# Expert stage of a fused two-block kernel: products split two blocks ahead, one-hots queued behind the products, and a longer pause in the top-k

## The chip, the core and the metric

The kernel runs on one core of a Trainium2 chip. The metric is device time in microseconds (us) of one launch, lower is better; three runs and one profiled execution of the kernel before are given. TensorE is called PE, VectorE DVE, ScalarE ACT, GpSimd POOL.

## The reference, cut to what matters

The program is one transformer block with three mixers and an expert stage, and then two blocks of another kind with four mixers and a feed-forward each. All of it is f32, for 256 tokens of width 1024. The change touches the expert stage alone:

```python
q = (h @ w_q).reshape(b, s, 8, 2, 128)
sc = einsum('bshpc,hpkc->bshpk', q, sub_keys)        # 8 heads x 2 halves x 128 keys
top_v, top_i = top_k(sc, 16)
cand_v = top_v[..., 0, :, None] + top_v[..., 1, None, :]   # 16 x 16 pairs of a head
best_v, best_pos = top_k(cand_v, 16)                 # 16 of 128*128 experts, for each head
gate = softmax(best_v)
act = gelu(einsum('chkd,cd->chk', u_tab[idx], h))
out = einsum('chk,chkd->cd', gate * act, v_tab[idx])
```

## The kernel before, in words

**Everything dense.** Nothing is gathered. The kernel computes act = gelu(U h) for all 16384 experts, as 128 blocks of 128 experts by 256 tokens, a matrix G of gates for all of them (zero for experts that were not picked), and then the sum over blocks of V^T (G * act). The first index of an expert is its block, 0 to 127, the second its row in the block. An f32 product is made of three matmuls on split operands (`mm3`, lines 178 to 180): high part times high part, high times low, low times high. A split is an ACT copy into a rounded type (the high part, line 191) and a DVE subtraction (the low part, line 192).

**Weights.** `Stream` loads weights by DMA on SP and hands them out in slots of eight 128 x 128 blocks. `_slot` splits a slot: `whi` on ACT (line 93), `wlo` on DVE or, where `pool_share` says so, on POOL (line 96). These have high priority, and there are three slots of each. One slot feeds 24 matmuls of 256 columns: one block of U (`u_block`, which ends in a gelu on ACT, line 773), or one block of V (`v_cols` for eight output columns).

**Order.** The scheduler orders each engine's queue at compile time, by priority (order in the program, weights earlier) among the instructions whose inputs it takes to be ready. Each engine runs its queue in order. `issue_after(x)` puts what a block traces on x's engine behind x in that queue; it is an order of issue and no wait. Background work is a generator (`add`). `blks` ticks once for every two weight blocks, so four times a slot; `yield n` asks for the next step after n ticks, rounded up, and `_step` puts the step's PE work behind the last matmul so far. `finish` runs all remaining steps of a task at once.

**Stages of `peer`.** (1) `topk`: eight units (four head pairs by two token halves) are searched on DVE, one per `TK_PACE` = 22 ticks, while PE runs blocks of U (`u_while`) and POOL makes `wlo`. After the last unit it pauses `TK_LAST` ticks. Then `gates` (a DVE subtraction, line 1013; an exp on ACT, line 1015, with a table load; sums and `slg` on DVE, line 1018), 6 ticks, `turn` (PE transposes `ptk`, line 248), 4 ticks. The number of U blocks done by the end is `early`. (2) `build(0, early)`: gates of blocks 0 to 63, in 32 steps of eight tokens. A step makes one-hots on DVE (`e2` line 805, `e1` line 807, `m` = e1 times the gates line 810), multiplies them on PE (`pgb`, line 818, eight matmuls), copies one half on ACT (line 822), adds the other on DVE (line 825) and multiplies it into the acts already there (line 831), or stores it where the act comes later (line 835). `e2`, `e1` and `m` have two buffers each. Meanwhile PE runs 64 blocks of U. (3) `collapse` multiplies gates by late acts, four blocks at a time (line 862), beside `FILL` = 3 blocks of U; blocks done are then `done`. (4) The V loop over blocks b: `weighted(b)` splits G * act into `ga`, of which there are two, and `v_cols` multiplies. After each odd b one block of U runs while any is left. `build(HALF, done)` makes the gates of blocks 64 to 127 beside it, a step per 10 ticks; `weighted(64)` calls `finish` on it, since it needs all tokens.

Of the kernel before, what the change touches and what calls it, by code (L numbers as in the profile page):

```python
# [8 lines left out]
F32R = mybir.dt.float32r  # L9
# [4 lines left out]
ALU = mybir.AluOpType  # L14
# [5 lines left out]
P = 128  # L20
S = 256
# [7 lines left out]
N_HA = 96  # L29
HALF = 64  # L30
TK_PACE = 22
TK_LAST = 48
FILL = 3
T_OH = 8
PACE = {0: 7.5, HALF: 10}
# [2 lines left out]
NBLK = 128  # L38
LAST = 3
# [93 lines left out]
class Core:  # L133
# [614 lines left out]
    def peer(self):  # L748
# [4 lines left out]
        tc, nc, a, ws = self.tc, self.nc, self.a, self.ws  # L753
        with ExitStack() as st:
            p = st.enter_context(tc.tile_pool(name="pe", bufs=1))
            hh, hl = self.hh, self.hl
            i1 = p.tile([P, S], F16, tag="i1", name="i1")
            i2 = p.tile([P, S], F16, tag="i2", name="i2")
            gt = p.tile([P, 2, S], F16, tag="gt", name="gt")
            iot = p.tile([P, P, 2], F16, tag="iot", name="iot")  # L760
            ga = [p.tile([P, 2, S], F32R, tag=f"ga{i}", name="ga") for i in range(2)]
# [22 lines left out]
                u_while(self.topk(tp, i1, i2, gt, iot), HALF, HALF)  # L784
            with tc.tile_pool(name="peg", bufs=1) as gp:
                hb = gp.tile([P, NBLK - N_HA, S], F32, tag="hb", name="hb")
                ws.pool_share = (0, 1)
                n2, n1 = T_OH * P, T_OH * HALF
                e = self.tp.tile([P, 2, n2 + n1], F16, tag="ld", name="e", bufs=1)
                e2s = [e[:, i, 0:n2].rearrange("p (q c r) -> p q c r", c=P, r=2) for i in range(2)]  # L790
                e1s = [e[:, i, n2:n2 + n1].rearrange("p (q c r) -> p q c r", c=HALF, r=2) for i in range(2)]

                def build(c0, done):


                    nq = T_OH // 2

                    def onehots(i):
                        ts = slice(i * T_OH, i * T_OH + T_OH)

                        def bc(x, n):
                            return x[:, ts].rearrange("p (q r) -> p q r", r=2)[:, :, None, :].to_broadcast([P, nq, n, 2])
                        e2, e1 = e2s[i % 2], e1s[i % 2]
                        m = gp.tile([P, nq, 2, HALF, 2], F16, tag="e1g", name="e1g", bufs=2)
                        nc.vector.tensor_tensor(out=e2, in0=iot[:, None].to_broadcast([P, nq, P, 2]), in1=bc(i2, P),
                                                op=ALU.is_equal)
                        nc.vector.tensor_tensor(out=e1, in0=iot[:, None, c0:c0 + HALF].to_broadcast([P, nq, HALF, 2]),
                                                in1=bc(i1, HALF), op=ALU.is_equal)
                        for j in range(2):
                            nc.vector.tensor_tensor(out=m[:, :, j], in0=e1, in1=bc(gt[:, j, :], HALF), op=ALU.mult)  # L810
                        return e2, m

                    def products(i, e2, m):
                        for o in range(0, T_OH, 4):
                            pg = self.bg.tile([P, 4, 2, HALF], F32, tag="bg", name="pgb")
                            for t in range(4):
                                q, r = (o + t) // 2, t % 2
                                nc.tensor.matmul(pg[:, t], lhsT=e2[:, q, :, r], rhs=m[:, q, :, :, r],
                                                 start=True, stop=True)
                            ts = slice(i * T_OH + o, i * T_OH + o + 4)  # L820
                            tmp = self.scr("gs").rearrange("p (t c) -> p t c", c=HALF)
                            nc.scalar.activation(out=tmp, in_=pg[:, :, 0, :], func=AF.Copy)

                            w = min(done, c0 + HALF) - c0
                            nc.vector.tensor_tensor(out=tmp[:, :, 0:w], in0=tmp[:, :, 0:w], in1=pg[:, :, 1, 0:w],
                                                    op=ALU.add)
                            for b, t, c1, c2 in ((ha, 0, 0, N_HA), (hb, N_HA, N_HA, NBLK)):
                                k0, k1 = max(c1, c0), min(c2, c0 + w)
                                if k0 < k1:
                                    d = b[:, k0 - t:k1 - t, ts]  # L830
                                    nc.vector.tensor_tensor(out=d, in0=d, op=ALU.mult,
                                                            in1=tmp[:, :, k0 - c0:k1 - c0].rearrange("p t c -> p c t"))
                                k0, k1 = max(c1, c0 + w), min(c2, c0 + HALF)
                                if k0 < k1:
                                    nc.vector.tensor_tensor(
                                        out=b[:, k0 - t:k1 - t, ts], op=ALU.add,
                                        in0=tmp[:, :, k0 - c0:k1 - c0].rearrange("p t c -> p c t"),
                                        in1=pg[:, :, 1, k0 - c0:k1 - c0].rearrange("p t c -> p c t"))

                    n = S // T_OH  # L840
                    nxt = onehots(0)
                    yield PACE[c0]
                    for i in range(n):
                        cur = nxt
                        if i + 1 < n:
                            nxt = onehots(i + 1)
                        products(i, *cur)
                        yield PACE[c0]

                early = ahead  # L850
                u_while(self.add(build(0, early), unit=1), HALF + early, early)
                assert ahead >= HALF

                def collapse(b0):

                    cut = NBLK - N_HA
                    b1 = min(b0 + 4, HALF)
                    for b, k0, k1 in ((ha, b0, min(b1, cut)), (hb, max(b0, cut), b1)):
                        if k0 < k1:
                            o = HALF if b is ha else HALF - N_HA  # L860
                            with tc.issue_after(ws.on_vector):
                                nc.vector.tensor_tensor(out=ha[:, k0:k1, :], in0=ha[:, k0:k1, :],
                                                        in1=b[:, k0 + o:k1 + o, :], op=ALU.mult)

                def weighted(b, g):

                    if b == HALF:
                        self.finish(more)
                    src = h(b)
                    if b >= done:  # L870
                        with tc.issue_after(ws.on_vector):
                            nc.vector.tensor_tensor(out=src, in0=src, in1=h(b - done), op=ALU.mult)
                    self.split(g[:, 0, :], g[:, 1, :], src)
                    return g


                done = NBLK
                nxt = weighted(0, ga[0])
                late = list(range(early, HALF, 4))
                for i in range(FILL):  # L880
                    for b in late[i * len(late) // FILL:(i + 1) * len(late) // FILL]:
                        collapse(b)
                    u_block(ahead, h(ahead))
                    ahead += 1
                done = ahead
                more = self.add(build(HALF, done), unit=1)
                acc = [pool.tile([P, 2, S], F32, tag=t, name="acc")
                       for pool, t in ((self.mm, "mm"), (self.bg, "bg")) for _ in range(2)]

                def v_cols(c, b, g, first, last):  # L890

                    wh, wl = ws.blks(("v", 0, 0), b, c)
                    self.mm3(acc[c // 2][:, c % 2, :], wh, wl, g[:, 0, :], g[:, 1, :],
                             first and c % 2 == 0, last and c % 2 == 1)

                for b in range(NBLK - LAST):
                    cur = nxt
                    if b + 1 < NBLK - LAST:
                        nxt = weighted(b + 1, ga[(b + 1) % 2])
                    for c in range(KD):  # L900
                        v_cols(c, b, cur, b == 0, False)
                    if b % 2 and ahead < NBLK:
                        u_block(ahead, h(ahead - done))
                        ahead += 1
                assert ahead == NBLK
                tl = self.tp.tile([P, LAST, 2, S], F32R, tag="ld", name="tail", bufs=1)
                tail = [weighted(NBLK - LAST + i, tl[:, i]) for i in range(LAST)]
            with tc.tile_pool(name="per", bufs=1) as gp:
# [6 lines left out]
                for c in range(KD):  # L915
                    for i, g in enumerate(tail):
                        v_cols(c, NBLK - LAST + i, g, False, i == LAST - 1)
                    if c % 2:
                        for d in (c - 1, c):
                            xc = self.x[:, d, :]  # L920
                            nc.vector.scalar_tensor_tensor(out=xc, in0=acc[d // 2][:, d % 2, :], scalar=1.0 / G_SCALE,
                                                           in1=xc, op0=ALU.mult, op1=ALU.add)
# [720 lines left out]
```

## Time and profile before

| | us |
|---|---|
| median of 3 runs | 2073.24 |
| lowest, highest run | 2063.41, 2077.04 |
| profiled execution, its time | 2076.68 |
| profiled execution, its span | 2074.9 |
| top-k beside U blocks | about 308 to 490 |
| `build(0)` beside U blocks (first to last `pgb`) | 500.05 to 685.84 |
| V loop | 694 to 1125 |
| of it with `build(HALF)` (first to last `pgb`) | 703.93 to 942.94 |

The span is the time from the first to the last instruction of the profile; the profiled execution's time is 1.8 us longer. A row of a timeline is start, duration, engine, line, operation, output<-inputs, shapes, count, and in brackets how long the engine sat idle before it and what it waited for. Ends of matmuls are modelled, so the distance of starts tells more than durations.

### The profile page before, as it was taken

The page shows a single profiled execution, that of the slowest core. Times are in us where ns is not written, and L with a number is a line of the kernel's source. Part 1 is how long each engine was busy: PE and PEld are TensorE (multiplying, and loading weights), DVE is VectorE, ACT ScalarE, POOL GpSimd, SP SyncE. Part 2 cuts the span into 40 slices and gives each one's busy share as a digit, 9 for nine tenths or more (in the row PEclk, how much of TensorE's full clock was granted, in tenths as well). Part 3 has the DMA queues.
Part 4 walks back from the last instruction along what each step waited for, and adds up shares of the span by engine and source line. Part 5 has one row for each costly group of instructions (what it writes and reads, how often), then busy time and mean ns, then how long its engine had stood idle before and what let it go on. Part 6 is the DMA issues. An engine that isn't in the chain of part 4 may idle for free.

```text
span 2074.9 us, 41467 instructions
## 1 busy us (share of the span) xinstructions
PE 2022.9 (97%) x16818; PEld 1966.0 (95%) x16818; DVE 1680.6 (81%) x3290; ACT 1158.1 (56%) x1906; POOL 265.4 (13%) x169
## 2 busy tenths in 40 slices
PE   8999999998999999999999999999999999999999
PEld 7989999998999999889999989999999989999997
DVE  7877779999999999886567999977555999977554
ACT  5688654445555555444556665466545666466543
POOL 2201207881000000000000111200000111200000
PEclk9999999999999999999999999999999999999999
DMA  6444555454544444444554643555555644554554
GB/s 213 143 132 170 199 204 173 173 183 143 183 168 178 167 179 178 148 164 163 202 184 182 221 148 142 199 184 187 199 199 188 226 158 144 197 189 166 202 201 152
DMA packets 57019, 370.01 MB, mean 178 GB/s; under 512 B 6587, under 2 KB 10236, under 8 KB 13564
## 3 DMA queue, kind: packets, MB, share of 16 engines
q1 hardware_dynamic: 50256, 357.06, 47.9%
q10 hardware_dynamic: 6572, 10.31, 1.7%
q8 instruction: 131, 2.15, 0.4%
q14 instruction: 60, 0.49, 0.1%
HBM read 364.73 MB, written 2.62 MB: 177 GB/s over the span
## 4 chain that ended last, share of the span: by engine, by line
PE 69%; DVE 19%; ACT 2%; issue 2%; POOL 0%; ACTq 0%; DVEq 0%; POOLq 0%
PE mm L180 5%; PE mm L178 5%; PE mm L179 5%; PE acc L179 5%; PE acc L180 5%; PE acc L178 5%; PE pu L178 4%; PE pu L179 4%; PE pu L180 3%; PE pg L180 3%; PE pg L178 3%; PE pg L179 3%; DVE wlo L96 3%; PE pp L180 2%; PE pp L179 2%; PE pp L178 2%
## 5 line engine op out<-in xcount | busy, mean ns | idle before, releaser
L93 ACT ACTIVATE whi<-raw 128x1024 fp32r<-128x1024 f32 x677 | 717.1, 1060 | 756.9 <-PE acc L179 174.0
L96 DVE TENSOR_TENSOR wlo<-raw,whi 128x1024 fp32r<-128x1024 f32 x622 | 769.1, 1237 | 299.4 <-ACT whi L93 297.6
L178 PE MATMUL pu<-hh,whi 128*128 128x256 f32 x1024 | 290.6, 284 | 6.7 <-ACT whi L93 6.7
L180 PE MATMUL pu<-hh,wlo 128*128 128x256 f32 x1024 | 286.3, 280 | 1.8 <-POOL wlo L96 1.8
L180 PE MATMUL mm<-hh,wlo 128*128 128x256 f32 x1008 | 281.6, 280 | 6.0 <-DVE wlo L96 6.0
L179 PE MATMUL pu<-hl,whi 128*128 128x256 f32 x1024 | 286.4, 280 | 0.0
L178 PE MATMUL mm<-hh,whi 128*128 128x256 f32 x1008 | 281.7, 280 | 0.0
L179 PE MATMUL mm<-hl,whi 128*128 128x256 f32 x1008 | 281.0, 279 | 0.0
L179 PE MATMUL acc<-ga,whi 128*128 128x256 f32 x1000 | 267.5, 281 | 10.0 <-DVE ga L192 10.0
L180 PE MATMUL acc<-ga,wlo 128*128 128x256 f32 x1000 | 264.6, 279 | 0.0
L178 PE MATMUL acc<-ga,whi 128*128 128x256 f32 x1000 | 233.6, 280 | 3.9 <-ACT ga L191 3.9
L179 PEld LDWEIGHTS acc<-ga,whi 128*128 128x128 f32 x1000 | 188.9, 189 | 13.0 <-DVE ga L192 13.0
L178 PEld LDWEIGHTS pu<-hh,whi 128*128 128x128 f32 x1024 | 194.0, 189 | 7.2 <-ACT whi L93 7.1
L180 PEld LDWEIGHTS mm<-hh,wlo 128*128 128x128 f32 x1008 | 190.9, 190 | 9.1 <-DVE wlo L96 7.8
L178 PE MATMUL pg<-hh,whi 128*128 128x256 f32 x704 | 197.7, 281 | 0.2 <-ACT gth L622 0.2
L180 PE MATMUL pg<-hh,wlo 128*128 128x256 f32 x704 | 197.0, 280 | 0.2 <-DVE wlo L96 0.2
L179 PE MATMUL pg<-hl,whi 128*128 128x256 f32 x704 | 196.8, 280 | 0.0
L180 PEld LDWEIGHTS pu<-hh,wlo 128*128 128x128 f32 x1024 | 194.8, 190 | 2.1 <-POOL wlo L96 2.1
L179 PEld LDWEIGHTS pu<-hl,whi 128*128 128x128 f32 x1024 | 193.7, 189 | 0.0
L178 PEld LDWEIGHTS mm<-hh,whi 128*128 128x128 f32 x1008 | 190.9, 189 | 1.2 <-issue 0.7
L179 PEld LDWEIGHTS mm<-hl,whi 128*128 128x128 f32 x1008 | 190.9, 189 | 1.1 <-issue 0.8
L180 PEld LDWEIGHTS acc<-ga,wlo 128*128 128x128 f32 x1000 | 188.6, 189 | 0.0
(413 smaller groups left out, 4862.8 us busy)
## 6 DMA issues: line engine op xcount, KB each, us to landing
raw<-in_w SPq DMA_DIRECT2D x336, 1024.0 KB
raw<-in_w SPq DMA_DIRECT2D x5, 512.0 KB
bias<-bias_scr ACTq DMA_DIRECT2D x4, 512.0 KB
bias_scr<-sbb ACTq DMA_DIRECT2D x16, 96.0 KB
cl<-in_cstl ACTq DMA_DIRECT2D x2, 576.0 KB
x<-in_xT SPq DMA_DIRECT2D x4, 256.0 KB
memt<-in_memT ACTq DMA_DIRECT2D x1, 1024.0 KB
keys<-in_keysT ACTq DMA_DIRECT2D x1, 1024.0 KB
```

The lines of the kernel that those rows point to most:

```text
L93: self.on_scalar = nc.scalar.activation(out=hi, in_=src, func=AF.Copy).ins
L96: i = eng.tensor_tensor(out=lo, in0=src, in1=hi.bitcast(F32), op=ALU.subtract)
L178: mm(out, lhsT=wh, rhs=xh, start=start, stop=False)
L179: mm(out, lhsT=wh, rhs=xl, start=False, stop=False)
L180: self.on_pe = mm(out, lhsT=wl, rhs=xh, start=False, stop=stop).ins
```

## The change

- `TK_LAST` goes from 48 to 64 ticks.
- A third `ga` buffer. `weighted` is called for block 1 ahead of the V loop and for block b + 2 at the head of iteration b (before: block b + 1).
- In a build step the products of step i come first in the program, then the one-hots of step i + 1 (before: the other way round), and the `e2` comparison of step i + 1 is queued behind the last DVE instruction of the products of step i. `e1` and `m` get no such tie.

```diff
-TK_LAST = 48
+TK_LAST = 64
...
+                ga.append(gp.tile([P, 2, S], F32R, tag="ga2", name="ga"))
...
+                    used = []
...
                         m = gp.tile([P, nq, 2, HALF, 2], F16, tag="e1g", name="e1g", bufs=2)
-                        nc.vector.tensor_tensor(out=e2, in0=iot[:, None].to_broadcast([P, nq, P, 2]), in1=bc(i2, P),
-                                                op=ALU.is_equal)
+                        with ExitStack() as st:
+                            if used:
+                                st.enter_context(tc.issue_after(used[-1]))
+                            nc.vector.tensor_tensor(out=e2, in0=iot[:, None].to_broadcast([P, nq, P, 2]),
+                                                    in1=bc(i2, P), op=ALU.is_equal)
...
-                                    nc.vector.tensor_tensor(out=d, in0=d, op=ALU.mult,
-                                                            in1=tmp[:, :, k0 - c0:k1 - c0].rearrange("p t c -> p c t"))
+                                    used.append(nc.vector.tensor_tensor(
+                                        out=d, in0=d, op=ALU.mult,
+                                        in1=tmp[:, :, k0 - c0:k1 - c0].rearrange("p t c -> p c t")).ins)
...
-                        cur = nxt
+
+                        products(i, *nxt)
                         if i + 1 < n:
                             nxt = onehots(i + 1)
-                        products(i, *cur)
...
-                nxt = weighted(0, ga[0])
+                ready = [weighted(0, ga[0])]
...
+                ready.append(weighted(1, ga[1]))
                 for b in range(NBLK - LAST):
-                    cur = nxt
-                    if b + 1 < NBLK - LAST:
-                        nxt = weighted(b + 1, ga[(b + 1) % 2])
+                    if b + 2 < NBLK - LAST:
+                        ready.append(weighted(b + 2, ga[(b + 2) % 3]))
+                    cur = ready.pop(0)
```

## Rows read from the trace of the kernel before

**Rows 1.** The page, busy time of each engine over the whole span.
```profile
PE 2022.9 (97%) x16818; PEld 1966.0 (95%) x16818; DVE 1680.6 (81%) x3290; ACT 1158.1 (56%) x1906; POOL 265.4 (13%) x169
```

**Rows 2.** Waits of PE, 475 to 1130: total us, times, longest.
```profile
PE acc L179 <- DVE ga L192: 10.0, 15, 1.1
PE pu L178 <- ACT whi L93: 6.7, 2, 6.0
PE acc L178 <- ACT ga L191: 3.9, 1, 3.9
PE pu L180 <- POOL wlo L96: 1.8, 1, 1.8
```

**Rows 3.** Windows: length, busy us (instructions) by engine, granted clock, DMA share, GB/s.
```profile
425.00:450.00 25.00, 25.00 (x214) 25.00 (x213) 24.73 (x65) 11.87 (x18) 20.19 (x10) 1.00 0.47 169
475.00:500.00 25.00, 17.48 (x126) 16.82 (x126) 23.95 (x60) 11.81 (x22) 7.67 (x3) 0.80 0.37 127
525.00:675.00 150.00, 150.00 (x1404) 149.11 (x1403) 142.22 (x301) 80.39 (x152) 0.00 (x0) 1.00 0.49 176
825.00:925.00 100.00, 91.89 (x818) 89.09 (x818) 87.80 (x205) 48.72 (x86) 0.00 (x0) 1.00 0.44 159
```

**Rows 4.** Timeline of ACT at the end of the top-k.
```profile
470.16 1.28 ACT L1015 ACT_TABLE_LOAD   x1
478.92 0.31 ACT L1015 ACTIVATE ge<-ge 128x128 f32<-128x128 f32 x1 [7.47 <-DVE ge L1013]
```

**Rows 5.** Timeline of PE at the end of the top-k.
```profile
480.23 0.58 PE L178 MATMUL pu<-hh,whi 128*128 128x256 f32 x1 [6.02 <-ACT whi L93]
...
489.89 0.33 PE L248 MATMUL ptk<-cst,slg 128*128 128x128 f32 x1 [0.52 <-DVE slg L1018]
```

**Rows 6.** Timeline of DVE, last two units of the top-k.
```profile
455.76 2.31 DVE L978 TENSOR_TENSOR cd<-tv 128x128 f32<-128x128 f32 x1
...
476.11 0.27 DVE L978 TENSOR_TENSOR cd<-tv 128x128 f32<-128x128 f32 x1
...
478.61 0.27 DVE L1013 TENSOR_TENSOR ge<-bv 128x128 f32<-128x128 f32 x1
```

**Rows 7.** Timeline of PE, gate products of both builds.
```profile
679.85 0.63 PE L818 MATMUL pgb<-e1g,e 128*128 128x128 f16 x8
...
685.84 0.63 PE L818 MATMUL pgb<-e1g,e 128*128 128x128 f16 x8
...
703.93 0.64 PE L818 MATMUL pgb<-e1g,e 128*128 128x128 f16 x8
...
825.53 0.64 PE L818 MATMUL pgb<-e1g,e 128*128 128x128 f16 x8
...
933.56 0.63 PE L818 MATMUL pgb<-e1g,e 128*128 128x128 f16 x8
...
939.55 0.63 PE L818 MATMUL pgb<-e1g,e 128*128 128x128 f16 x8
```

**Rows 8.** Timeline of DVE, the last steps of the first build, and collapse.
```profile
680.52 0.69 DVE L805 TENSOR_TENSOR e<-iot,i 128x1024 f16<-128x1024 f16 x1 [0.31 <-PE pgb L818]
681.12 0.75 DVE L810 TENSOR_TENSOR e1g<-e,gt 128x512 f16<-128x512 f16 x2
...
683.82 0.41 DVE L807 TENSOR_TENSOR e<-iot,i 128x512 f16<-128x512 f16 x1
...
684.99 1.22 DVE L96 TENSOR_TENSOR wlo<-raw,whi 128x1024 fp32r<-128x1024 f32 x1
...
690.98 4.95 DVE L862 TENSOR_TENSOR ha<-ha,hb 128x1024 f32<-128x1024 f32 x5
```

**Rows 9.** Timeline of DVE, products of a step at the end of the second build.
```profile
941.87 0.36 DVE L825 TENSOR_TENSOR gs<-gs,pgb 128x200 f32<-128x200 f32 x1
...
943.53 0.27 DVE L831 TENSOR_TENSOR hb<-hb,gs 128x72 f32<-128x72 f32 x1
```

**Rows 10.** Waits of DVE, 475 to 1130: total us, times, longest.
```profile
DVE e L805 <- PE pgb L818: 30.6, 53, 1.7
```

More of the change, by code (lines that the diff above doesn't have):

```diff
@@ L830, in products @@
                                     d = b[:, k0 - t:k1 - t, ts]
-                                    nc.vector.tensor_tensor(out=d, in0=d, op=ALU.mult,
-                                                            in1=tmp[:, :, k0 - c0:k1 - c0].rearrange("p t c -> p c t"))
+                                    used.append(nc.vector.tensor_tensor(
+                                        out=d, in0=d, op=ALU.mult,
+                                        in1=tmp[:, :, k0 - c0:k1 - c0].rearrange("p t c -> p c t")).ins)
                                 k0, k1 = max(c1, c0 + w), min(c2, c0 + HALF)
                                 if k0 < k1:
-                                    nc.vector.tensor_tensor(
+                                    used.append(nc.vector.tensor_tensor(
                                         out=b[:, k0 - t:k1 - t, ts], op=ALU.add,
                                         in0=tmp[:, :, k0 - c0:k1 - c0].rearrange("p t c -> p c t"),
-                                        in1=pg[:, :, 1, k0 - c0:k1 - c0].rearrange("p t c -> p c t"))
+                                        in1=pg[:, :, 1, k0 - c0:k1 - c0].rearrange("p t c -> p c t")).ins)
                     n = S // T_OH
```

## The prediction

> **What bounds the kernel now.** The page first: PE is busy for 97% of the span [rows 1], so no other engine bounds the kernel as a whole, and a change of order can win only the time in which PE waits or runs slow. The waits of PE between 475 and 1130 come next, since the change touches that stretch alone [rows 2]. They sum to 22.9 us with the 0.5 us before the transposes [rows 5], 1.1% of the time, and have three places. At the end of the top-k PE waits 6.0 + 1.8 us for split weights and 0.5 us for `slg`. In the V loop it waits 10.0 us in 15 pieces for the low part of `ga`. At the end of the second build it waits 3.9 us for the high part of `ga`. The windows add what waits don't show [rows 3]: from 475 to 500 the granted clock is 0.80, so part of that stretch ran at 1.2 GHz instead of 2.4. Its 126 matmuls take 17.48 busy us, where at the 25/214 = 0.117 us of 425 to 450 they would take 14.7; the low clock costs 2.8 us. All that could be won is thus about 26 to 28 us, 1.3%.
>
> Then the places. In the first build gate products start 5.99 us apart (679.85, 685.84) and PE has no wait; DVE is busy for 142.2 of 150 us, 5.68 us of a step [rows 3, 7]. In the second build the first 16 steps, with U blocks between V blocks, take (825.53 - 703.93)/16 = 7.60 us. The next 13, where only V blocks are left, take (933.56 - 825.53)/13 = 8.31 us [rows 7]. That is 0.71 us a step, 9.2 us in all, and nearly the 10.0 us of waits. From 825 to 925 DVE is busy 87.8%, so 0.878 x 8.31 = 7.30 us a step: under the 7.60 that PE needs, with 4% to spare. What holds DVE up is order: `e2` is queued right behind a `pgb` that PE has not run yet, 53 times, 30.6 us [rows 10].
>
> **The longer pause.** 16 ticks are 32 weight blocks, four blocks of U, 4 x 24 x 0.117 = 11.2 us on PE. Now ACT loads the exp table at 470.16 and sits until 478.92 for the subtraction that DVE starts at 478.61 [rows 4, 6]; the weight copy behind the exp comes late, and PE stands from 474 to 480.23 [rows 5]. With the pause the exp can start at 470.16 + 1.28 + 11.2 = 482.6. DVE will be later too. POOL, which makes the low parts of weights, ran dry while PE stood; in the unit before it did not, and the same addition `cd` took 2.31 us there and 0.27 us here [rows 6]. So I take the subtraction at 478.61 + 2.04 = 480.7, and the exp finds it done. What is late next is `slg` for the transposes: 489.89 - 478.61 = 11.3 us after the subtraction [rows 5, 6], at 492.0. PE reached the transposes at 489.89 - 0.52 = 489.4; without the 7.8 us of waits and 2.8 us of slow clock, and with 11.2 us more of blocks, that is 490.0. I allow 1 us for weight copies behind the table loads on ACT (half idle, rows 3). PE then waits 1 us for `slg`. New loss 2.0 us and 0.5 of clock, old loss 8.3 + 2.8 = 11.1: **8.6 us won**. Bounds: 11.1 if nothing is late; a loss of 4 if DVE comes much later (rival below).
>
> Here a rule of the skill bears on it. With POOL running, `cd` took 2.31 instead of 0.27 us [rows 6]. The Trainium skill (GPSIMD Engine Reference, section Key points) says that GpSimd shares its SBUF interfaces with VectorE, so that VectorE instructions with two SBUF inputs, or in a two-port mode, contend with it. It speaks against a longer pause, since POOL goes on splitting weights through DVE's last and densest work. By my rows part of these instructions is held, as now; by the rule all would be, and the 8.6 us won would become some 4 us lost, as in rival (3).
>
> **What else the pause moves.** Four more U blocks are done at the end of the top-k: 51, not 47. The step of `gs` in the second build covers 200 = 4 x 50 columns [rows 9], so 114 blocks are done when it starts; it becomes 118. Ten U blocks, not 14, are left to stand between V blocks. PE's total is unchanged. One collapse of 1024 columns goes: five take 4.95 us, the last of them a quarter [rows 8], so one is 1.1 us. The longest wait for `ga` in rows 2, 1.1 us, is the one behind them at the start of the V loop: **1.1 us won**, bounds 0 and 1.8. The pieces of a gate step get 16 columns wider or narrower, some hundredths of a us, within DVE's idle.
>
> **Two blocks ahead.** Both before and after, `ga` of a block can be split when its buffer comes free, at the end of block b - 1; but now it is wanted a block of 24 matmuls, some 2.7 us, later. Each wait in rows 2 is 1.1 us or less, so that cover ends all, as long as DVE keeps up: 7.30 of 7.60 us a step. ACT issues the same copies earlier. Of the 9.2 us I leave 2 to DVE's small reserve: **7.2 us won**, bounds 9.2 and a loss of 2 (second build at 8.0 us a step, below).
>
> **One-hots behind products.** This takes `e2` from the head of DVE's queue behind a `pgb` and puts it after the products, 0.6 us less between `pgb` and products. `e1` and `m` are not tied, and `m` too must wait until the earlier `pgb` has read its buffer; it can keep part of the 30.6 us. No queue but DVE's is reordered; behind the tied `e2` stand weight splits and `ga`. In steady state I cost it at nothing, hidden by 0.3 us of DVE reserve in either build.
>
> **The end of the second build.** `weighted(64)` now comes at block 62, not 63, and four U blocks fewer lie before it: 72 slots or 288 ticks, where it was 77 or 308. Products of step i come at tick 11 + 10i, so 28 steps are done, not 30, and four are run off at once, not two. Now two take from 939.55 to the end of the 3.9 us wait, 7.9 us; PE has 24 matmuls and two `pgb` groups to do, 2.7 + 0.9 (a group 0.44), and so stands 3.9 [rows 2, 7]. For four: products 943.80 - 941.87 = 1.93 us each [rows 9], 7.7; one-hots of three steps, each 0.69 + 0.75 + 0.41 less overlaps, 1.6 [rows 8], 4.8, and the tie keeps them in line; two weight splits 2.3 [rows 8]; start and last split 1.3: 16.1 us. PE has 48 matmuls and four groups, 7.2 us, and stands 8.9: 5.0 more, and half a us of low clock: **5.5 us lost**. Bounds: 1 lost if splits fit in gaps and the next blocks cover, 9 lost if each step pays a round trip to PE and ACT.
>
> **The sum.** 8.6 + 1.1 + 7.2 - 5.5 = 11.4 us. On the profiled execution's 2076.7 us (span 2074.9 and 1.8 around it) that gives 2065.3; the median of the runs lies 3.4 us lower, at 2073.2, and gives 2062. I forecast 2062 us, own range 2054 to 2070.
>
> **The rivals.**
> (1) Slower: the one-hots come late. In the first build products end at 684.99, 5.14 us after their `pgb` at 679.85, and the next DVE instruction is a weight split [rows 7, 8]. Without `e2` in front that is 4.53; if the split (high priority) stays ahead of the tied `e2`, `e2` is ready at 4.53 + 1.14 + 0.69 = 6.36 us, and the next `pgb`, due at 5.99, waits 0.37. 31 times that is 11.5 us. The second build would go at 8.0 us in 28 steps, 11 us lost instead of 9.2. Sum 8.6 + 1.1 - 2 - 5.5 - 11.5: 9 us slower, 2082. It decides whether a split stands between products and `e2`. For it: DVE has 5% to spare. Against: the reserve is positive, and PE can take `pgb` a few matmuls later.
> (2) All is won: the four last steps hide behind blocks 62 and 63 and DVE keeps up. 11.4 + 5.5 + 2 + 2: 21 us faster, 2052. Against: 16 us of DVE work beside 7 of PE.
> (3) DVE is held throughout: the one-hots of the last unit run beside POOL. If five of its instructions after the subtraction are each held as `cd` was, 2.04 us [rows 6], `slg` comes 10 us later. PE waits 11 us at the transposes, with 1 more ahead and 2.8 of clock: 15 for 11.1, so -4 for +8.6. Sum -1: 2074. Against: DVE is as busy from 425 to 450, with POOL at work for 20 of 25 us, and PE never waited there [rows 3].
> (4) The tie doesn't do what it says: `m` takes `e2`'s place behind `pgb`, DVE goes on at 7.30 + 1.0 us, and the V steps stay at 8.3. 8.6 + 1.1 - 5.5: 4 us faster, 2069.
>
> **How the numbers follow.** Forecast 0.46, rival (1) 0.13, (2) 0.17, (3) 0.07, (4) 0.17. One per cent, 21 us, is about what a measurement of this kernel can tell from no change. Faster by more than that takes rival (2) and a little beyond, 0.14; slower by more takes rival (1) with both builds at its upper end, 0.07; within 1% 0.79. The range, 2047 to 2083, takes in (2), (3), (4), most of (1), and the 7 us by which single runs lie around the median.
>
> **What would show it.** No wait of ACT for `ge` and a wait of 0 to 3 us before `ptk`, with a full clock from 475 to 500. First-build steps at 5.99 us; 6.2 or more is rival (1). Second-build steps at 7.6 to the end; 8.3 is rival (4). Four short steps at its end, and one wait of 7 to 10 us of PE for `ga`; under 4 is rival (2). The forecast is wrong if PE waits for `e2` in every step, or if the wait at the top-k's end has only moved to the transposes.

## The result, and the profile after

The changed kernel takes 2057.9 us, the median of 15 runs (2045.03 to 2071.58); beside it the kernel before took 2072.74 (2063.41 to 2085.85, 15 runs). The ratio is 0.9931, with a 95% interval of 0.9909 to 0.9953: 14.3 us faster, between 9.8 and 18.9. The forecast was 2062 with an own range of 2054 to 2070 and a gain of 11.4. Sign and size of the sum came out as forecast, but several of its terms did not, and their errors nearly cancelled.

The profiled execution of after took 2051.29 us, 25.4 less than that of before. The page of after, span and busy time, stands against [rows 1]:

```profile
span 2049.5 us, 41488 instructions
...
PE 2006.7 (98%) x16818; PEld 1952.2 (95%) x16818; DVE 1673.3 (82%) x3281; ACT 1159.0 (57%) x1906; POOL 277.9 (14%) x173
```

PE runs the same 16818 matmuls in 16.2 us less of busy time and stands 9 us less. The waits of PE from 475 to 1130 answer to [rows 2]; columns: engine, tile and line, what it waited for, total us, times, longest.

```profile
PE pgb L823 <- DVE e L810: 5.8, 2, 3.5
PE acc L178 <- ACT ga L191: 2.3, 1, 2.3
PE pu L180 <- POOL wlo L96: 2.1, 1, 2.1
...
PE acc L179 <- DVE ga L192: 1.1, 1, 1.1
PE ptk L248 <- DVE slg L1025: 1.1, 1, 1.1
PE pu L178 <- ACT whi L93: 1.1, 2, 0.6
```

Three things to see. The 15 waits for the low part of `ga` have become one, of 1.1 us. Of the 6.0 us for `whi` at the end of the top-k 0.5 is left; `wlo` and `slg` are late there by 2.1 and 1.1. And a new line heads the list: PE waits 5.8 us for one-hots, with 2.3 us for `ga` behind it. The timelines say where. ACT at the end of the top-k [rows 4]: the subtraction now comes 0.42 us after ACT is free for the exp, not 7.47.

```profile
472.64 1.28 ACT L1022 ACT_TABLE_LOAD   x1
474.35 0.31 ACT L1022 ACTIVATE ge<-ge 128x128 f32<-128x128 f32 x1 [0.42 <-DVE ge L1020]
```

PE there [rows 5], then gate products of the second build [rows 7], then its end:

```profile
475.66 0.39 PE L178 MATMUL pu<-hh,whi 128*128 128x256 f32 x1 [0.47 <-ACT whi L93]
...
478.24 0.38 PE L180 MATMUL pu<-hh,wlo 128*128 128x256 f32 x1 [2.08 <-POOL wlo L96]
...
485.34 0.33 PE L248 MATMUL ptk<-cst,slg 128*128 128x128 f32 x1 [1.13 <-DVE slg L1025]
...
700.75 0.63 PE L823 MATMUL pgb<-e1g,e 128*128 128x128 f16 x8
...
818.41 0.63 PE L823 MATMUL pgb<-e1g,e 128*128 128x128 f16 x8
...
891.94 0.63 PE L823 MATMUL pgb<-e1g,e 128*128 128x128 f16 x8
...
899.29 0.63 PE L823 MATMUL pgb<-e1g,e 128*128 128x128 f16 x8
...
906.31 0.63 PE L823 MATMUL pgb<-e1g,e 128*128 128x128 f16 x8
...
911.28 0.63 PE L823 MATMUL pgb<-e1g,e 128*128 128x128 f16 x8
...
915.38 0.64 PE L823 MATMUL pgb<-e1g,e 128*128 128x128 f16 x8 [3.46 <-DVE e L810]
...
918.35 1.03 PE L823 MATMUL pgb<-e1g,e 128*128 128x128 f16 x8 [2.34 <-DVE e L810]
...
921.69 0.58 PE L178 MATMUL acc<-ga,whi 128*128 128x256 f32 x1 [2.31 <-ACT ga L191]
```

The first 16 steps take (818.41 - 700.75)/16 = 7.35 us, the next ten (891.94 - 818.41)/10 = 7.35, and so does the one from 891.94 to 899.29: the steps beside V blocks alone (V-only steps below) no longer take longer than those with U between them. Then come four short steps, and PE stands 3.46 + 2.34 + 2.31 = 8.1 us before block 64. That is the run-off of the four steps that `finish` runs all at once. The windows of after show its clock [rows 3]:

```profile
475.00:500.00 25.00, 21.33 (x172) 20.54 (x170) 22.46 (x38) 14.21 (x27) 7.68 (x3) 0.93 0.49 169
...
900.00:925.00 25.00, 16.89 (x143) 16.20 (x143) 21.86 (x62) 9.51 (x20) 0.00 (x0) 0.82 0.45 165
```

The granted clock from 475 to 500 is 0.93, where it was 0.80. From 900 to 925, about the run-off, it is 0.82.

**Where the 25.4 us between the profiles lie.** The starts of PE's instructions cut both traces at the same places. The table also has another execution of the kernel before, profiled for the first experiment below (span 2065.7):

| stretch of PE, us | before | before, again | after |
|---|---|---|---|
| start to the last scores (`sc`) | 423.68 | 415.79 | 415.64 |
| to the first `pgb` (after: four U blocks more) | 76.37 | 76.83 | 79.84 |
| first build, first to last `pgb` | 185.79 | 185.79 | 187.27 |
| to the first `pgb` of the second build | 18.09 | 19.64 | 18.00 |
| to the end of the wait before block 64 (after: four U blocks fewer) | 243.53 | 239.53 | 220.94 |
| the rest of the span | 1127.4 | 1128.2 | 1127.8 |

In the stretch that the change touches (second to fifth row) 523.78 us became 506.05, a gain of 17.7; against the other execution of before it is 15.7. The remaining 8 us of the first pair lie ahead of the last scores, where no edit reaches; the second execution of before is faster there by the same 8 us. So nearly a third of what the first pair of profiles shows is not the change.

### The profile page after: what moved, and what is told of

It is laid out like the page before. It is cut to its first block, busy times and chain, and to the rows that moved or that the text cites. A ratio compares the mean times of both kernels' runs of the same rounds, so it can differ in the third digit from the quotient of the medians.

```text
span 2049.5 us, 41488 instructions
## 1 busy us (share of the span) xinstructions
PE 2006.7 (98%) x16818; PEld 1952.2 (95%) x16818; DVE 1673.3 (82%) x3281; ACT 1159.0 (57%) x1906; POOL 277.9 (14%) x173
## 4 chain that ended last, share of the span: by engine, by line
PE 68%; DVE 19%; issue 2%; ACT 2%; DMA 1%; ACTq 0%; DVEq 0%
PE acc L178 5%; PE acc L179 5%; PE acc L180 5%; PE mm L178 5%; PE mm L179 5%; PE mm L180 5%; PE pu L180 3%; PE pu L178 3%; PE pu L179 3%; PE pg L180 3%; PE pg L178 3%; PE pg L179 3%; DVE wlo L96 3%; PE pp L180 2%; PE pp L179 2%
## 5 line engine op out<-in xcount | busy, mean ns | idle before, releaser
L178 PE MATMUL pu<-hh,whi 128*128 128x256 f32 x1024 | 285.2, 278 | 1.1 <-ACT whi L93 1.1
L178 PE MATMUL acc<-ga,whi 128*128 128x256 f32 x1000 | 277.4, 280 | 2.3 <-ACT ga L191 2.3
L179 PE MATMUL acc<-ga,whi 128*128 128x256 f32 x1000 | 277.5, 278 | 1.1 <-DVE ga L192 1.1
L180 PE MATMUL acc<-ga,wlo 128*128 128x256 f32 x1000 | 276.6, 278 | 0.0
L179 PEld LDWEIGHTS acc<-ga,whi 128*128 128x128 f32 x1000 | 189.8, 190 | 1.3 <-DVE ga L192 1.3
L178 PEld LDWEIGHTS acc<-ga,whi 128*128 128x128 f32 x1000 | 188.1, 189 | 2.6 <-ACT ga L191 2.6
```

The lines of the kernel that those rows point to most:

```text
L178: mm(out, lhsT=wh, rhs=xh, start=start, stop=False)
L179: mm(out, lhsT=wh, rhs=xl, start=False, stop=False)
L180: self.on_pe = mm(out, lhsT=wl, rhs=xh, start=False, stop=stop).ins
```

## The experiments

Each part alone, each part left out, and then the term that was lost. Ratios are to the kernel before, run beside each on the same chip (2071.08 in the first set, 2077.32 in the second, 2078.06 in the third).

**The kernel before once more**, no edit.

> The kernel before, unchanged, once more. Theory M (matmul pace): the profiled execution before ran its matmuls some 4% slower from 200 to 475 and from 703 to 825 than elsewhere, with no wait to show for it; if that is chance of one execution, the second execution has its slow stretches in other places, and the first 16 steps of the second build take 7.35 us instead of 7.60. Theory O (order): the 7.60 us belong to the kernel, and come back. In both, the last 12 steps with only V blocks take 8.2 to 8.5 us, and the top-k ends with waits of PE of 7 to 9 us.

Measured: 2067.53 us. At the top-k's end PE waits 8.3 + 1.8 + 1.2 = 11.3 us, 3 more than in the first profile of the same kernel. The V-only steps take what they took, 8.13 to 8.53 us, with the same waits (10.2 us, 15 times, for the low part of `ga`). But the 16 steps ahead of them take 7.35 us, not 7.60:

```profile
698.05 0.63 PE L818 MATMUL pgb<-e1g,e 128*128 128x128 f16 x8
...
705.40 0.63 PE L818 MATMUL pgb<-e1g,e 128*128 128x128 f16 x8
...
824.13 0.63 PE L818 MATMUL pgb<-e1g,e 128*128 128x128 f16 x8
...
832.65 0.63 PE L818 MATMUL pgb<-e1g,e 128*128 128x128 f16 x8
```

So the base from which the prediction measured the loss of a V-only step, 7.60, belonged to that execution and not to the kernel. The last section comes back to it.

**The longer pause alone.**

```diff
-TK_LAST = 48
+TK_LAST = 64
```

> The kernel before with the longer pause alone. My theory: the wait of ACT for the exp falls from 7.5 us to under 1, the waits of PE at the end of the top-k from 8.3 us to about 3.7, the low clock there costs 1 us less; four U blocks fewer in the V loop bring some 5 more steps of the second build into the stretch with only V blocks, at 0.7 us each, and one more step to run off at the end (3.5 us). Net 0 to 2 us gained, ratio 0.998 to 1.002. Rival: the pause is what made the change fast, 6 us or more, ratio 0.997 or less.

Measured: 2073.45 us, ratio 1.0001 (0.9978 to 1.0024): nothing. Its trace shows why. At the top-k's end PE waits 4.5 + 1.8 + 0.3 = 6.5 us, where the two profiles of before have 8.3 and 11.3. The collapse that went took its 1.1 us wait along. But V-only steps begin four U blocks earlier, after 11 steps instead of 16, so 17 steps are stretched instead of 13, and four steps are run off (6.35 us of waits instead of 3.9). What the pause wins ahead of the build is given back in it. (This execution took 2088.84 us, the longest of the 12, and its first build ran at 6.19 us a step, so only its waits and its second build are compared here.)

**The third buffer and two blocks ahead alone.**

```diff
+                ga.append(gp.tile([P, 2, S], F32R, tag="ga2", name="ga"))
...
-                nxt = weighted(0, ga[0])
+                ready = [weighted(0, ga[0])]
...
+                ready.append(weighted(1, ga[1]))
...
-                    cur = nxt
-                    if b + 1 < NBLK - LAST:
-                        nxt = weighted(b + 1, ga[(b + 1) % 2])
+                    if b + 2 < NBLK - LAST:
+                        ready.append(weighted(b + 2, ga[(b + 2) % 3]))
+                    cur = ready.pop(0)
```

> The kernel before with the third buffer and the split two blocks ahead alone. Theory cover: the waits of 0.6 to 0.75 us for the low part of ga go, since each is shorter than the block that is gained, and the steps with only V blocks fall from 8.3 to about 7.4 us; one more step runs off at the end; net 6 us faster, ratio 0.997. Theory order: DVE still stands behind the gate products with its e2, needs 7.3 us of work and 1 of standing for a step, and the steps stay at 8.0 us or more; net 0 or slower, ratio 1.000 to 1.002.

Measured: 2054.54 us, ratio 0.9925 (0.99 to 0.995): the whole gain of the change, 15.5 us. Waits of PE and of DVE, 475 to 1130:

```profile
PE pu L178 <- ACT whi L93: 9.8, 2, 9.2
PE acc L178 <- ACT ga L191: 3.9, 1, 3.9
PE pu L180 <- POOL wlo L96: 1.8, 1, 1.8
PE acc L179 <- DVE ga L192: 1.2, 1, 1.2
...
DVE e L806 <- PE pgb L819: 15.7, 44, 1.0
```

The theory of cover is borne out, but it expected 6 us (0.997), less than half of it. The waits inside the V loop are gone (the 1.2 us left are at its start), and its steps are 7.35 us to the end, although `e2` stands behind `pgb` as before, 44 times and 15.7 us. From the first `pgb` of this build to the end of the wait before block 64 it takes 227.0 us, where the second execution of before takes 239.5: 12.5 us by the traces. The waits at the top-k's end (9.2 + 1.8) and the run-off of two steps (3.9) are those of before.

**The tie and the new order alone.**

```diff
+                        with ExitStack() as st:
+                            if used:
+                                st.enter_context(tc.issue_after(used[-1]))
...
-                        cur = nxt
+
+                        products(i, *nxt)
                         if i + 1 < n:
                             nxt = onehots(i + 1)
-                        products(i, *cur)
```

> The kernel before with the new order of products and one-hots and the tie alone, two ga buffers and the short pause as before. Theory order: DVE's standing behind gate products falls from 30 us to under 5, and the steps with only V blocks fall to 7.4 to 7.7 us, ratio 0.996 to 0.998. Theory cover: the waits of PE for the low part of ga stay at 0.6 us and more a step, the steps at 8 us or more, ratio 1.000.

Measured: 2079.2 us, ratio 1.0035 (1.001 to 1.0061): a little slower. Waits of PE and DVE, then V-only steps:

```profile
PE acc L179 <- DVE ga L192: 10.2, 15, 1.3
...
DVE e1g L814 <- PE pgb L822: 18.9, 22, 1.7
```

```profile
825.02 0.63 PE L822 MATMUL pgb<-e1g,e 128*128 128x128 f16 x8
...
832.26 0.39 PE L179 MATMUL acc<-ga,whi 128*128 128x256 f32 x1 [0.64 <-DVE ga L192]
...
833.52 0.63 PE L822 MATMUL pgb<-e1g,e 128*128 128x128 f16 x8
```

DVE's stand behind `pgb` fell from 30.6 us to 18.9, and `m` (printed `e1g`) has it now. PE's waits didn't move, and a V-only step is still 833.52 - 825.02 = 8.50 us. But the stand fell in the first build (10.3 us to 1.0), where PE doesn't wait. Over the 13 V-only steps it stayed. The same line of before (825.5 to 933.5), of this run (816.5 to 924.7) and of the third buffer alone (817.6 to 913.2):

```profile
DVE e L805 <- PE pgb L818: 12.5, 12, 1.7
...
DVE e1g L814 <- PE pgb L822: 12.4, 12, 1.7
...
DVE e L806 <- PE pgb L819: 1.5, 6, 0.5
```

So this run doesn't tell what DVE would do there without the stand. The third buffer does tell that the old order can stay: with it the stand went by itself. In the first build three steps became longer: 6.67, 6.22 and, the last, 6.56 us instead of 5.99.

**The change without the tie.**

```diff
-                        with ExitStack() as st:
-                            if used:
-                                st.enter_context(tc.issue_after(used[-1]))
...
-                        products(i, *nxt)
                         if i + 1 < n:
                             nxt = onehots(i + 1)
+                        products(i, *cur)
```

> The changed kernel without the tie and with the old order of products and one-hots (longer pause and third buffer alone). My theory now: the third buffer is the whole gain in the V loop, and the tie adds nothing, since DVE's standing behind gate products cost PE time only through ga. Then the steps of the second build stay at 7.35 us, the first build keeps 5.99 us from its first step to its last (1.5 us less than with the tie), and the ratio to before is 0.991 to 0.994, not above that of the change. Rival: the tie shortens the run-off of four steps at the end or frees DVE for it; without it PE waits there more than 8.1 us and the ratio is 0.995 or more.

Measured: 2059.79 us, ratio 0.9912 (0.9877 to 0.9947), no worse than the whole change. The run-off costs 6.35 us of waits, where with the tie it is 8.1; the wait of 1.1 us ahead of the V loop is gone, where with the tie it stayed; the first build's steps are 5.99 throughout. Its second build ran at 7.60 us a step from the first to the last of the paced ones.

**The change with the pause of 48.**

```diff
-TK_LAST = 64
+TK_LAST = 48
```

> The changed kernel with the old pause of 48 ticks. My theory: the pause gives some 5 to 7 us at the end of the top-k and takes as much at the end of the second build, so this one loses 8 to 11 us in waits at the top-k and only 3 to 4.5 us at the end of the second build (two steps run off), and the ratio to before is 0.991 to 0.995, the same as the change. Rival: the pause is worth its 6 us and the end of the build costs nothing more; then 0.996 or more.

Measured: 2065.98 us, ratio 0.9953 (0.9927 to 0.9979). Run-off 0.5 + 3.6 us; steps 7.35. At the top-k's end PE waits only 2.1 + 2.6 us here, and not the 8 to 11 expected, so the gap that the pause was to close was half as wide in this execution as in the others. The ratio lies between the theory's 0.995 and the rival's 0.996; it decides for neither.

**The change without the third buffer.**

```diff
-                    if b + 2 < NBLK - LAST:
-                        ready.append(weighted(b + 2, ga[(b + 2) % 3]))
-                    cur = ready.pop(0)
+                    cur = nxt
+                    if b + 1 < NBLK - LAST:
+                        nxt = weighted(b + 1, ga[(b + 1) % 2])
```

> The changed kernel without the third buffer, blocks split one ahead as before. My theory: the steps with only V blocks are back at 8.2 to 8.5 us, about 16 of them, with a wait for ga in each, in spite of the tie; ratio to before 1.000 to 1.004. Rival: with the pause and the tie together DVE keeps up without the buffer, steps at 7.6 or less, ratio 0.996 or less.

Measured: 2078.05 us, ratio 1.0003 (0.9977 to 1.003): the gain is gone. From the 12th step on each takes 8.18 to 8.56 us, in spite of the tie, and the waits of PE are back:

```profile
PE acc L179 <- DVE ga L192: 12.3, 18, 0.8
PE pgb L822 <- DVE e L809: 6.2, 3, 3.4
PE acc L178 <- ACT ga L191: 2.3, 1, 2.3
```

With that, all eight combinations of the three parts have been run:

| ratio to before | two `ga` buffers | three `ga` buffers |
|---|---|---|
| pause 48, old order | 1 | 0.9925 |
| pause 64, old order | 1.0001 | 0.9912 |
| pause 48, tie | 1.0035 | 0.9953 |
| pause 64, tie | 1.0003 | 0.9931 (0.9906 when run again) |

Along each row the third buffer wins 0.0072 to 0.0097: 15 to 20 us, whatever else is done. The tie loses 0.0035, 0.0028, 0.0002 and 0.0019 (or wins 0.0006 by the second figure): small, and only the first of them, against before itself, is clear of its interval. The pause wins between 0 and 0.0047.

**Nine ticks a step.** The run-off is a matter of count: at ten ticks 28 of 32 steps are done when `weighted(64)` wants all of them. At nine, 31 fit in the 288 ticks (11 + 9 x 30 = 281). Pause 64 and third buffer, old order, and:

```diff
-PACE = {0: 7.5, HALF: 10}
+PACE = {0: 7.5, HALF: 9}
```

> Longer pause and third buffer, old order, and a step of the second build every 9 ticks instead of 10. A step then stands beside 54 matmuls (6.12 us) and 8 short ones (0.44), 6.6 us of PE, against some 6.9 us of DVE. If DVE's work between the end of the first build and block 64 is what bounds that stretch, the wait before block 64 falls from 8 us to 4 or less and short waits come back in the steps instead, together 1 to 3 us less than with 10 ticks; ratio 0.990 to 0.993. Rival: DVE falls behind by more than two blocks cover, steps of 7.2 us and over with waits for ga in each, and the ratio is 0.995 or more.

Measured: 2049.83 us, ratio 0.9864 (0.9825 to 0.9904). A window over the steps, then the end of the build:

```profile
705.00:905.00 200.00, 200.00 (x1861) 198.96 (x1860) 199.66 (x478) 109.74 (x195) 0.00 (x0) 1.00 0.50 178
```

```profile
905.21 0.63 PE L819 MATMUL pgb<-e1g,e 128*128 128x128 f16 x8
911.89 0.63 PE L819 MATMUL pgb<-e1g,e 128*128 128x128 f16 x8
918.80 0.39 PE L179 MATMUL acc<-ga,whi 128*128 128x256 f32 x1 [0.31 <-DVE ga L192]
```

The run-off is gone; one wait of 0.31 us is left. PE is busy for all 200 us, and DVE for 199.66, where in the same window of after it is 194.10. DVE has nothing to spare, but PE doesn't notice: the short waits that the theory wanted in the steps did not come, and the ratio is below its 0.990. On the same chip the kernel with ten ticks, which is the change without the tie, ran from 2051.3 to 2062.88, this one from 2043.7 to 2054.31. From the first `pgb` of this build to the end of the last wait it is 213.8 us, against 220.94 in after.

**The changed kernel once more**, no edit, beside the next three.

> The changed kernel, unchanged, beside the next three on the same chip. Ratio to before 0.991 to 0.995 as in its first measurement. In its profile matmuls keep one of two paces (113 or 118 ns) over long stretches, in other places than in the first profile; the four steps run off at the end of the second build cost PE 7 to 9 us of waits again, and the waits of PE at the end of the top-k lie anywhere from 1 to 8 us, by how many of DVE's instructions POOL holds up there.

Measured: 2059.97 us, ratio 0.9906 (0.9872 to 0.994). Waits at the top-k's end 1.4 + 2.7, in the run-off 3.4 + 2.2 + 2.3 = 7.9 us, the first two steps of the first build 6.9 and 6.4 for 5.99. Steps of the second build take 7.60 us throughout, where the first profile of the same kernel has 7.35.

**The change with nine ticks.**

```diff
-PACE = {0: 7.5, HALF: 10}
+PACE = {0: 7.5, HALF: 9}
```

> The changed kernel, tie and all, with a step of the second build every 9 ticks. If the tie is of no account here either, it equals the version without it: ratio to before 0.985 to 0.990, no run-off at the end, steps of 6.7 us. If the tie costs where DVE has no reserve, PE waits for e2 in the steps, they take 6.9 us and over, and the ratio is 0.990 or more.

Measured: 2053.03 us, ratio 0.9873 (0.9827 to 0.9919), 7 us under the changed kernel on the same chip, though the intervals overlap. The run-off is a wait of 0.57 us.

**Nine ticks and a pause of 80**, old order.

```diff
-TK_LAST = 64
+TK_LAST = 80
```

> Third buffer, old order, a step every 9 ticks, and a pause of 80 ticks. The waits of PE at the end of the top-k go to 0 to 2 us whatever POOL holds up. Four more U blocks leave the V loop; where DVE is busy for 99.8% of the time already, each block that goes leaves PE 0.34 us of DVE work more for its slot, and one step more has to be done by block 64. My theory: that gives 5 us back, about the same time as with 64 ticks, ratio 0.985 to 0.990. Rival: DVE falls behind for good, PE waits in each step and 5 us or more before block 64, ratio 0.991 or more.

Measured: 2054.28 us, ratio 0.9877 (0.9831 to 0.9923). The wait at the top-k's end falls to 0.75 us. Four U blocks fewer before block 64 leave 272 ticks, enough for 30 steps (11 + 9 x 29 = 272), and the run-off is back with 3.3 + 2.7 us. Steps reach 8.2 us near the end. The rival's sign, 5 us or more before block 64, thus came, but not its ratio. A longer pause only pays while the build still gets done.

**Nine ticks and four U blocks ahead of the V loop**, pause 64, old order.

```diff
-FILL = 3
+FILL = 4
```

> Third buffer, old order, a step every 9 ticks, pause of 64 ticks, and four U blocks instead of three while DVE collapses late acts. The waits of 0.6 us and more at the start of the V loop go; one U block leaves the V loop. Within 2 us of the version with three, ratio 0.985 to 0.990.

Measured: 2047.13 us, ratio 0.985 (0.9803 to 0.9896): by its median the fastest of all, 31 us under before and 13 under the changed kernel on the same chip. From the variant with `FILL` = 3 it can't be told apart. The wait of 0.64 us at the start of the V loop, which was to go, is there in both. Its profile has only 0.7 us of wait at the top-k's end; since the top-k is the same as in that variant (7.8 us there), this is not the fill's doing.

## Why the prediction was right, and where it was not

**Two blocks ahead: forecast 7.2 us, and the whole gain.** The cause was named rightly: a split that is wanted one block of 24 matmuls later is no longer waited for, and 14 of rows 2's 15 waits went together. The size was off. In both executions of before 13 V-only steps take 108.0 us, and at the 7.35 of after they take 95.6: 12.4 us. The step that failed is the base of 7.60, read from 16 steps of one profile; from there only 9.2 us could be lost, and of those 2 were held back for DVE. The V-only steps themselves ran at the shorter of the two paces of the last section (matmuls 113 to 114 ns apart in both executions), so 7.35 is their base. Nor was the reserve of 2 needed, though DVE has less to spare than the 4% of the prediction: in the V-only steps of the third buffer alone it is busy for 56.19 of 57 us (833 to 890), and PE for all 57. The waits of rows 2 were too small a measure as well: some 0.7 us a step are listed, but a step fell by 0.96. A wait starts at the modelled end of the matmul before; by its start, the matmul behind a listed 0.63 us (841.17) comes 0.91 us after the one before instead of 0.11, and the next 0.22.

**"What holds DVE up is order" was half of a loop.** It was a reading of rows 10, and it cost nothing in the sum only because the tie was costed at nothing. With the tie alone, V-only steps stayed at 8.2 to 8.5 us and `m` took over the whole stand there, 12.4 us for 12.5, as rival (4) has it. With the buffer alone, the order being the old one, the stand fell to 1.5 us and the steps to 7.35. In the V-only steps of before each engine waited for the other: DVE's 7.3 us of work and its stand of 0.96 (12.5 us over 13 steps) make up nearly the whole step of 8.31, and PE, late for want of `ga`, came late to the next `pgb`. In such a loop the trace can't tell which wait is the cause. The buffer opened it. Whether an order that moves `m` as well would have opened it too was not run. A third of rows 10, 10.3 us in the first build, is of order alone; it cost nothing, since PE waits for nothing there. Rival (4) thus had the mechanism of the tie right and its consequence wrong: the V steps did not need the tie.

**The tie: forecast 0.** Three small costs appear with it: three longer steps of the first build wherever it stands (187.27 instead of 185.79, 1.5 us), and beside the pause of 64 some 1 us ahead of the V loop (below) and 1.6 to 1.8 us in the run-off of four steps (7.9 to 8.1 instead of 6.35). Some 4 us in all, the size of the mean of the four pairs of ratios (0.0021, 4.4 us). The pairs themselves don't follow it: those with the pause of 48, where the traces show some 2 us, differ most. So the size of the tie's cost stays uncertain. Rival (1), `e2` late in every step, did not come: 28 steps of the first build stay at 5.99, and PE waits for `e2` only in the run-off. (In two later profiles with the tie, the change once more and the change with nine ticks, PE also waits for it in three steps of the first build, 1.3 and 2.1 us.)

**The longer pause: forecast 8.6.** The exp finds its subtraction nearly done, `wlo` and `slg` are late next, as forecast; PE waits 3.7 us instead of 2.0 and the clock stays at 0.93. In the pair with the second execution of before the stretch is worth 10.9 - 3.0 = 7.9 us (four U blocks, 96 matmuls at 0.1133 us, less the 3.0 by which it is longer). Over all executions it is less. The waits there, five with 48 ticks: 8.3, 11.3, 11.0, 11.0, 4.7 us, mean 9.3; eight with 64: 3.7, 6.5, 6.2, 1.4, 7.8, 4.1, 4.1, 0.7, mean 4.3. The pause wins 5.0 us of waits, where 6.3 of the forecast 8.6 were waits (8.3 to 2.0) and the rest the clock. By the whole stretch, in which the clock counts, the five have a mean of 75.9 us (71.3 to 77.7) and the eight, less 10.9, of 70.3 (65.1 to 73.6): 5.5 us won, not 8.6. The term was mis-sized. What varies is DVE's search. From the first scores to the subtraction of the last unit it takes, for the eight with 64 ticks, beside PE's waits there:

| DVE, us | 163.7 | 166.3 | 171.3 | 174.7 | 174.7 | 175.7 | 175.7 | 175.8 |
|---|---|---|---|---|---|---|---|---|
| PE waits, us | 1.4 | 0.7 | 3.7 | 4.1 | 4.1 | 6.5 | 6.2 | 7.8 |

In five executions with 48 ticks it took 164.7 to 170.4. The forecast of DVE being 2 us later holds for the mean (172 against 168, so 4), but a single execution moves it by 12. In each of them 32 to 39 of the search's 501 DVE instructions (weight splits left out) took over 1.1 us, as `cd` did in rows 6; every one of these ran beside an instruction of POOL. So rival (3), DVE held throughout and 11 us of wait at the transposes, did not come: with 64 ticks PE waits there for 2.7 us at most. The Trainium skill (GPSIMD Engine Reference, section Key points) says that GpSimd and VectorE contend for shared SBUF interfaces; these rows agree in kind, and show that the contention takes a varying part of the instructions.

**One collapse less: forecast 1.1, then 0.** Without the tie the wait did go (pause alone, change without tie). With it 0.7 to 1.1 us stay (and 0.5 with nine ticks): the tie took the gain back, and the forecast had taken the two as independent.

**The run-off: forecast -5.5.** Four steps, one group of waits, 8.1 us against 8.9 forecast; 4.2 us more than the 3.9 of before, 4.8 in the stretch. (From the second execution of before to after the fifth row of the table falls by 18.6: 10.9 of moved blocks and 12.4 of V-only steps, less 4.8.) Rival (2), all won, fell here.

**The sum.** By that pair of profiles 7.9 + 12.4 - 4.8 - 1.5 = 14.0, the last term being the tie's in the first build (the gap behind that build, 1.6 us shorter in after, makes it the 15.7 of the table). With the mean of 5.5 for the pause it is 11.6. Measured: 14.3, 9.8 to 18.9. Forecast: 11.4. That it came so near is luck: the V loop was put 5.2 us too low and the run-off 0.7 too dear, while the pause was put 3.1, the tie 1.5 and the collapse 1.1 us too high. That the pause alone is worth nothing (1.0001) is the more telling number: 5 us and a collapse of 1.1 won, 2.5 lost in the run-off, and four more V-only steps that lose about a microsecond each.

## What to carry to other kernels

An engine that waits a little in every block for a split made one block ahead is helped by one more buffer, before any reordering: it alone gave the whole of these 15 us, with the suspicious order of the other engine left as it was. Work that is paced in the background and run off at a deadline should be counted out (steps by ticks): one tick less per step (0.9912 to 0.9864) was worth more than the pause and the tie together (0.9925 to 0.9931, or 0.9906 when run again). And a step length taken as a base should come from two executions.

## What the runs showed of the hardware

Matmuls of the same shape run at two paces, with no wait and no lower clock to show for it. The same window over blocks of U, in the first and the second execution of the kernel before:

```profile
220.00:280.00 60.00, 60.00 (x512) 60.00 (x511) 40.74 (x55) 31.91 (x44) 6.71 (x6) 1.00 0.64 217
```

```profile
220.00:280.00 60.00, 60.00 (x532) 60.00 (x532) 42.02 (x59) 31.88 (x45) 5.78 (x5) 1.00 0.66 224
```

PE is busy for all 60 us in both, the granted clock is 1.00 (the 2.4 GHz level), and one does 512 matmuls where the other does 532. From start to start the matmuls of 256 columns stand 117.8 and 113.3 ns apart. A pace can hold for hundreds of microseconds, and the stretches lie elsewhere in each of two executions of the same kernel. Some changes lie at a stall of PE (at about 698 and 832 us in the first profile of before), others have none near. It is the difference of 7.60 and 7.35 us a step, in both kernels (after: 7.35 in one profile, and in the other:)

```profile
704.76 0.64 PE L823 MATMUL pgb<-e1g,e 128*128 128x128 f16 x8
...
712.36 0.64 PE L823 MATMUL pgb<-e1g,e 128*128 128x128 f16 x8
```

From 200 us to the last scores the first profile of before ran nearly all at the longer pace and the second nearly all at the shorter. By the starts of the same matmuls the first falls 6.4 us behind there, most of the 8 us ahead of the last scores. By these numbers a kernel at one pace throughout would differ by an estimated 3.9% from the same at the other; the 15 executions of after spread by 26.6 us (1.3%). What sets the pace wasn't settled: no run was made for it.
